# Other hold times for the exponential and the sines of the state-space parameters

## The chip, the cores and the metric

The kernel runs on one core of a Trainium2 chip. The metric is the device time of one execution in microseconds (us), lower is better. Inside a core five engines work side by side, each through its own queue in order: TensorE (PE; its weight loads are shown as PEld), VectorE (DVE), ScalarE (ACT), GpSimd (POOL) and SyncE (SP), which here only starts DMA transfers.

## The reference

The reference is a trunk of two decoder layers over 256 tokens of width 2048, in float32. Each layer normalises the input, multiplies it by one wide input matrix, and hands the columns to three mixers: a latent attention (MLA), a diagonal complex state-space layer (S5), and a dilated window attention. Their outputs are normalised, go through an output matrix, and are followed by a gated feed-forward part. What matters here is the discretisation of the state-space layer, whose parameters have 32 values per partition for both layers:

```
lam  = complex(min(a_re, -1e-4), a_im)
dt   = exp(log_dt)
a_bar = exp(lam * dt)
b_bar = ((a_bar - 1) / lam) * b
h_t  = a_bar * h_(t-1) + b_bar * u_t        # associative scan over the tokens
y    = Re(c . h) + d_skip * u
```

So the real part of `lam * dt` needs an exponential, and its imaginary part, an angle, needs sines and cosines.

## The kernel before, in words

**Matrix products.** Every weight matrix is cut into stripes of up to 512 columns. A stripe is accumulated over row blocks k of 128 rows. For accuracy each operand is split into a high and a low half, and one row block takes six products on TensorE: three for each of the two token halves. Weights come by DMA in tiles of two row blocks (512 KB for a full stripe, ring `wr` of 4 buffers). ACT copies a tile into its high half `wh`, DVE subtracts to get the low half `wl` (method `wsplit`, rings of 4 buffers each). The loop in `run` keeps the splits three tiles ahead of the products. A stripe's accumulators `acc` are emptied when it ends (`done`).

**Order of layer 0.** `ORDER[0]` starts with the stripe `cq` (16 row blocks, tiles 0 to 7) and the stripe `u` (tiles 8 to 15), then `ckv`. `cq_done` queues four ACT instructions (a copy and a sum of squares for each token half); the transposes of that copy (group `latq0`) follow on TensorE inside the stripe `u`. `u_done` starts the state-space chain, group `ssm0`, which also needs the parameters of group `prep0`. Its result is wanted by the stripes `g1` and `g0`, near the end of the layer's mixers.

**The planner.** The whole program is one fixed order per engine, written out when the kernel is built. Class `Pace` carries a clock for each engine (lines 113 to 182) and adds a cost for each instruction: for POOL 2.5 ns for each of the 32 columns plus 165 ns, and 450 ns more while the planner's DVE clock is ahead of its POOL clock (line 141), with 90 ns between dependent POOL instructions (line 143). Side work is written as generators. Each `yield` gives the earliest planner time of the next step. Before each row block, `run_side` (line 289) issues a step if its time has come on the planner's TensorE clock and the engines aren't `busy` (line 281): in layer 0 DVE may be ahead of TensorE by at most 3500 ns, ACT by at most 4500 ns. These clocks decide the order alone; on the chip each engine takes its queue in that order and waits where an operand isn't there.

**The parameters.** `params` (line 467) first issues 76 POOL instructions at once, at the very start of the kernel. They produce, in this order: `x` (the exponent's argument), `f`, `fh`, `fl` (the angle in turns), a half-angle sine and cosine by polynomials, `d` (the squared modulus of `lam`), and last `fr` (the angle's fraction for 128 tokens). The rest stands behind three yields:

```
480        mid = self.pace.t["gpsimd"] + Pace.LAG        # x is done
518        yield max(mid, self.HOLD[0])
519        self.pexp(nc.vector, E, x, W[21:25], em1)
520        yield max(early, self.HOLD[1])                # early: fl is done
521        yield from self.angles(0, 0)
522        yield max(late, self.HOLD[2])                 # late: fr is done
523        nc.vector.reciprocal(d, d)
525        nc.scalar.activation(s8, fr, AF.Sin, scale=2 * math.pi)
527        nc.scalar.activation(c8, fr, AF.Sin, bias=self.halfpi, scale=-2 * math.pi)
528        self.sines(0)
```

`pexp` is 17 small DVE instructions, `angles` three steps of DVE instructions, and the step behind the third yield holds one DVE reciprocal, six ACT instructions (four sines and two absolute values, the first with a table load) and 16 POOL products that end in `cr` and `ci`. The next step of `prep0` issues two loads on SP (`load_c`, `load_b`), then `ssm_c` and `ssm_b` follow on DVE and ACT.

Of the kernel before, what the change touches and what calls it, by code (L numbers as in the profile page):

```python
# [207 lines left out]
class Trunk:  # L208
# [46 lines left out]
        self.side.append([gen, group, self.pace.end + Pace.TO_PE if ready is None else ready])  # L255

    WARM = (9, 10)
    HOLD = (27000.0, 0.0, 39000.0)

    TUNE = (dict(W=3, s=10000.0, d=12000.0, m=9000.0, AV=3500.0, AS=4500.0, SL=0.0),  # L260
            dict(W=2, s=7000.0, d=16000.0, m=4000.0, AV=3000.0, AS=3000.0, SL=150.0))
# [205 lines left out]
    def params(self):  # L467
# [49 lines left out]
        late = self.pace.t["gpsimd"] + Pace.LAG  # L517
        yield max(mid, self.HOLD[0])
        self.pexp(nc.vector, E, x, W[21:25], em1)
        yield max(early, self.HOLD[1])  # L520
        yield from self.angles(0, 0)
        yield max(late, self.HOLD[2])
        nc.vector.reciprocal(d, d)
# [891 lines left out]
```

## Time and profile before

| | |
|---|---|
| median of 3 runs | 2173.07 us (2170.6 to 2173.99) |
| the profiled execution, device time | 2171.57 us |
| its span, first to last instruction | 2169.8 us |
| TensorE busy | 2127.0 us, 98% |
| VectorE busy | 1314.2 us, 61% |
| ScalarE busy | 1048.0 us, 48% |
| GpSimd busy | 96.3 us, 4%, most of it in the first 60 us |
| mean granted TensorE clock | 0.995 of full speed |

An engine's rows give when an instruction started and how long it ran; a bracket gives the idle time just before it and what ended it. The names are those of the program without their numbers: `wr`, `wh`, `wl` are the weight tile and its halves, `pt` and `acc` PSUM tiles, `one` a tile that lives through the kernel, `s` all other tiles in SBUF.

### The profile page before, as it was taken

The numbers are of one execution on the slowest core, as the hardware profiler recorded it, in microseconds if no ns is written. First come the engines' busy times: TensorE is split into PE (matmuls) and PEld (weight loads), VectorE is DVE, ScalarE is ACT, GpSimd is POOL, SyncE is SP. The second block draws the span as 40 slices with busy tenths as digits, with TensorE's granted clock in tenths as the row PEclk, the third lists the DMA queues.
The fourth block names the chain that finished last, engine by engine and source line by source line (L and its number), as shares of the span: only waits on it lengthen the run. The fifth ranks groups of instructions, "written<-read, shape, count | busy, mean of one in ns | idle before, by whom it ended". The sixth has DMA issues, their size and how long they took to land.

```text
span 2169.8 us, 27761 instructions
## 1 busy us (share of the span) xinstructions
PE 2127.0 (98%) x10511; PEld 1765.5 (81%) x10511; DVE 1314.2 (61%) x1789; ACT 1048.0 (48%) x1529; POOL 96.3 (4%) x251
## 2 busy tenths in 40 slices
PE   9999979999999999999999999999999999999998
PEld 7887768888888888888888887888888888888886
DVE  7996767458544555445568785765545455544555
ACT  6667445446334444444455665564443444434443
POOL 7100000000000000000001000000000000000000
PEclk9999999999999999999999999999999999999999
DMA  7653435667666666666555444566666766666664
GB/s 239 190 168 116 143 101 167 200 195 232 190 193 190 192 186 194 195 187 191 184 159 153 126 128 137 176 182 191 179 196 194 212 183 194 192 194 193 184 186 145
DMA packets 201269, 388.41 MB, mean 179 GB/s; under 512 B 12064, under 2 KB 20512, under 8 KB 201136
## 3 DMA queue, kind: packets, MB, share of 16 engines
q1 hardware_dynamic: 199952, 382.39, 58.4%
q0 software_dynamic: 1184, 4.26, 0.6%
q8 instruction: 82, 1.34, 0.3%
q14 instruction: 51, 0.42, 0.1%
HBM read 384.51 MB, written 2.10 MB: 178 GB/s over the span
## 4 chain that ended last, share of the span: by engine, by line
PE 87%; DVE 5%; ACT 3%; POOL 2%; issue 2%; DMA 0%; DVEq 0%; ACTq 0%; POOLq 0%
PE acc L198 82%; PE pt L198 5%; DVE s L198 3%; ACT s L198 2%; DVE wl L198 2%; POOL s L198 1%; PE y L198 1%; ACT wh L198 1%; POOL one L198 0%; DVE tn L198 0%; DMA wr<-in_w_ukv_dram 0%; POOL tn L198 0%; DMA one<-in_params_dram 0%; ACT L198 0%; DVE one L198 0%
## 5 line engine op out<-in xcount | busy, mean ns | idle before, releaser
L198 PE MATMUL acc<-wh,s 128*128 128x512 f32 (+2 forms) x5760 | 1808.6, 390 | 12.7 <-ACT s L198 7.9
L198 DVE TENSOR_TENSOR wl<-wr,wh 128x1024 fp32r<-128x1024 f32 (+1 forms) x720 | 866.2, 1209 | 679.2 <-ACT wh L198 677.0
L198 PEld LDWEIGHTS acc<-wh,s 128*128 128x128 f32 x5760 | 1079.3, 188 | 231.3 <-ACT s L198 9.9
L198 PE MATMUL acc<-wl,s 128*128 128x512 f32 (+2 forms) x2880 | 1114.6, 387 | 3.7 <-DVE wl L198 3.7
L198 ACT ACTIVATE wh<-wr 128x1024 fp32r<-128x1024 f32 (+1 forms) x720 | 747.9, 1047 | 730.4 <-PE acc L198 701.4
L198 PEld LDWEIGHTS acc<-wl,s 128*128 128x128 f32 x2880 | 542.0, 188 | 109.1 <-DVE wl L198 6.2
L198 ACT ACTIVATE s<-pt 128x512 fp32r<-128x512 f32 (+5 forms) x122 | 65.0, 549 | 137.1 <-PE pt L198 136.8
L198 DVE TENSOR_TENSOR s<-pt,s 128x512 f32<-128x512 f32 (+1 forms) x108 | 71.1, 686 | 59.2 <-ACT s L198 54.2
L198 PE MATMUL pt<-one,s 128*128 128x128 f32 x668 | 98.1, 273 | 3.4 <-DMA s<-in_x_dram 1.5
L198 ACT ACTIVATE s<-s 128x512 f32<-128x512 f32 (+4 forms) x162 | 79.9, 503 | 44.2 <-DVE s L198 35.5
L198 PEld LDWEIGHTS pt<-one,s 128*128 128x128 f32 x668 | 81.0, 142 | 23.8 <-ACT s L198 3.1
L198 DVE TENSOR_TENSOR s<-s,s 128x512 f32<-128x512 f32 (+3 forms) x88 | 78.0, 905 | 4.7 <-ACT s L198 4.0
L198 ACT ACTIVATE s<-pt,tn 128x128 f32<-128x128 f32 (+2 forms) x128 | 44.1, 375 | 75.9 <-DVE tn L198 58.8
L198 ACT ACTIVATE s<-acc,one 128x512 f32<-128x512 f32 (+3 forms) x112 | 63.3, 608 | 28.1 <-PE acc L198 22.9
L198 ACT ACTIVATE s<-pt,one 128x256 fp32r<-128x256 f32 x108 | 45.9, 470 | 63.6 <-PE pt L198 63.4
L198 DVE SCALAR_TENSOR_TENSOR s<-pt,one,s 128x256 fp32r<-128x256 f32 x108 | 47.7, 478 | 43.5 <-ACT s L198 43.1
L198 DVE SCALAR_TENSOR_TENSOR s<-acc,one,s 128x512 f32<-128x512 f32 x92 | 64.5, 743 | 10.0 <-POOL one L198 10.0
L198 PE MATMUL pt<-s,s 128*128 128x128 f32 (+1 forms) x352 | 58.2, 296 | 3.8 <-ACT s L198 2.7
L198 PEld LDWEIGHTS pt<-s,s 128*128 128x128 f32 x352 | 49.9, 191 | 9.2 <-ACT s L198 4.5
L198 POOL TENSOR_TENSOR tn<-one 128x2 f32<-128x2 f32 x27 | 10.9, 402 | 1027.1 <-DVE one L198 1025.7
L198 DVE TENSOR_TENSOR_SCAN s<-s,s 128x512 f32<-128x512 f32 x32 | 38.8, 1218 | 0.3
L198 DVE TENSOR_TENSOR s<-acc,s 128x512 f32<-128x512 f32 (+1 forms) x57 | 36.3, 673 | 3.9 <-PE acc L198 3.9
(74 smaller groups left out, 396.5 us busy)
## 6 DMA issues: line engine op xcount, KB each, us to landing
wr<-in_w_gate_dram SPq DMA_DIRECT2D x176, 512.0 KB, 4.2
wr<-in_w_up_dram SPq DMA_DIRECT2D x176, 512.0 KB, 4.2
wr<-in_w_down_dram SPq DMA_DIRECT2D x176, 512.0 KB, 4.3
wr<-in_w_in_dram SPq DMA_DIRECT2D x80, 512.0 KB, 4.1
wr<-in_w_o_dram SPq DMA_DIRECT2D x64, 512.0 KB, 3.9
wr<-in_w_uq_dram SPq DMA_DIRECT2D x16, 384.0 KB, 3.6
wr<-in_w_in_dram SPq DMA_DIRECT2D x16, 320.0 KB, 3.1
s<-in_bT_dram SPq DMA_DIRECT2D x8, 512.0 KB, 5.0
```

The lines of the kernel that those rows point to most:

```text
L198: return f(out, *a, **k)
```

## The change

One line: the three hold times behind which `params` keeps its later steps. The first, for the exponential, goes from 27000 to 16000 ns of the planner's clock. The third, for the reciprocal and the sines, goes from 39000 to 0, so that `late`, the planner's own estimate of when `fr` is done, decides. The second was 0 and stays 0.

```diff
     WARM = (9, 10)
-    HOLD = (27000.0, 0.0, 39000.0)
+    HOLD = (16000.0, 0.0, 0.0)
```

No instruction is added or taken out by it. What each engine does first can change, from the exponential on.

## Rows read from the trace of the kernel before

**Rows 1.** The page, busy time of each engine over the span.
```profile
PE 2127.0 (98%) x10511; PEld 1765.5 (81%) x10511; DVE 1314.2 (61%) x1789; ACT 1048.0 (48%) x1529; POOL 96.3 (4%) x251
```
**Rows 2.** Stretches: length, then PE, PEld, DVE, ACT, POOL busy us (count), clock, DMA.
```profile
54.00:61.00 7.00, 7.00 (x41) 6.34 (x40) 6.78 (x14) 4.13 (x7) 5.65 (x10) 1.00 0.75 276
160.00:200.00 40.00, 38.97 (x250) 32.85 (x250) 22.69 (x47) 28.66 (x77) 1.94 (x6) 1.00 0.43 131
```
**Rows 3.** Timeline of POOL: start, us, instruction, count, and idle time before it.
```profile
6.00 0.30 POOL L198 TENSOR_SCALAR one<-one 128x32 f32<-128x32 f32 x1 [4.05 <-DMA one<-in_params_dram]
...
16.96 0.47 POOL L198 TENSOR_TENSOR s<-one,s 128x32 f32<-128x32 f32 x2
...
21.40 2.37 POOL L198 TENSOR_SCALAR one<-s 128x32 f32<-128x32 f32 x1
...
24.82 0.29 POOL L198 TENSOR_SCALAR s<-s 128x32 f32<-128x32 f32 x1
...
42.85 0.32 POOL L198 TENSOR_SCALAR s<-s 128x32 f32<-128x32 f32 x1
```
**Rows 4.** Timeline of ACT around the sines.
```profile
32.52 1.06 ACT L198 ACTIVATE wh<-wr 128x1024 fp32r<-128x1024 f32 x1 [1.65 <-PE acc L198]
34.56 0.69 ACT L198 ACTIVATE s<-acc,one 128x512 f32<-128x512 f32 x1 [0.98 <-DVE s L198]
...
36.62 0.63 ACT L198 ACTIVATE s<-s 128x512 f32<-128x512 f32 x1
...
41.57 1.28 ACT L198 ACT_TABLE_LOAD   x1
43.20 0.23 ACT L198 ACTIVATE one<-s 128x32 f32<-128x32 f32 x1 [0.35 <-POOL s L198]
...
45.76 1.04 ACT L198 ACTIVATE wh<-wr 128x1024 fp32r<-128x1024 f32 x1
```
**Rows 5.** Timeline of DVE around the exponential, and the last split before the sines.
```profile
19.69 1.65 DVE L198 SCALAR_TENSOR_TENSOR s<-pt,one,s 128x256 fp32r<-128x256 f32 x4
21.26 2.35 DVE L198 TENSOR_TENSOR wl<-wr,wh 128x1024 fp32r<-128x1024 f32 x2
...
31.34 0.66 DVE L198 TENSOR_SCALAR s<-s 128x32 f32<-128x32 f32 x3
...
35.23 1.23 DVE L198 TENSOR_TENSOR wl<-wr,wh 128x1024 fp32r<-128x1024 f32 x1
...
41.42 1.23 DVE L198 TENSOR_TENSOR wl<-wr,wh 128x1024 fp32r<-128x1024 f32 x1
```
**Rows 6.** Timeline of PE, the places that the steps are moved past.
```profile
24.39 0.39 PE L198 MATMUL acc<-wl,s 128*128 128x512 f32 x1
...
39.13 0.60 PE L198 MATMUL pt<-one,s 128*128 128x128 f32 x4
...
40.73 0.63 PE L198 MATMUL acc<-wh,s 128*128 128x512 f32 x2
```
**Rows 7.** Timeline of PE, waits behind the change; all waits of 60 to 90 us over 0.5.
```profile
62.14 0.41 PE L198 MATMUL acc<-wl,s 128*128 128x320 f32 x1 [0.55 <-DVE wl L198]
...
82.65 0.73 PE L198 MATMUL acc<-wh,s 128*128 128x512 f32 x2 [1.53 <-DVE s L198]
```
**Rows 8.** The clock after a short and after a longer gap of PE: stretches and PE's timeline.
```profile
82.00:84.00 2.00, 1.35 (x6) 1.14 (x7) 2.00 (x6) 1.32 (x2) 0.00 (x0) 1.00 0.62 198
230.00:232.00 2.00, 0.49 (x4) 0.16 (x2) 2.00 (x3) 1.64 (x9) 0.00 (x0) 1.00 0.00 0
232.00:234.00 2.00, 1.22 (x2) 0.50 (x2) 1.97 (x3) 0.54 (x3) 0.00 (x0) 0.53 0.69 165
...
238.00:240.00 2.00, 2.00 (x10) 1.58 (x9) 0.12 (x1) 1.84 (x3) 0.11 (x1) 0.77 0.03 8
...
232.60 0.80 PE L198 MATMUL acc<-wh,s 128*128 128x512 f32 x1 [2.10 <-ACT s L198]
...
299.10 2.36 PE L198 MATMUL y<-s,one 128*32 128x128 f32 x40 [6.81 <-DVE s L198]
```

## The prediction, made before the change was run

> **What bounds the kernel now.** I read the page first: TensorE is busy for 2127.0 of 2169.8 us [rows 1], so all other engines matter only where TensorE waits for them, about 43 us in all. Then came the timelines of the first 60 us, engine by engine, since the change touches nothing else directly. After the start-up, TensorE's first wait is the one before 62.14 [rows 7]. POOL works through the 76 parameter instructions from 6.00 to 43.17 us [rows 3]. ACT sets its sines behind the high halves of tile 12, loads the table at 41.57 and waits 0.35 us for POOL's last value `fr` until 43.20 [rows 4]. DVE does the exponential at 31.34, when it is two tiles ahead [rows 5]. So now the sines arrive almost exactly when POOL is done, and nobody is kept waiting. The reader is to see that arrival: any earlier place in ACT's queue is a wait until about 43 us.
>
> **Where the planner puts the steps now.** This is order, not time, and I carried the planner's clocks by hand from the cost lines. At 245 ns an instruction plus 90 ns between dependent ones its POOL chain has `x` at 11.3, `fl` at 15.4 and `fr` at 27.4 us of its clock, far ahead of the 43.17 of the chip [rows 3]. A row block counts 1.362 us. The exponential may now go from 16.0 on; at 16.77 DVE is 3.60 us ahead, more than the 3.5 allowed, so it goes in at 18.13, in front of `cq`'s row block 5 and of the low half of tile 4 (before: in front of block 12). It adds 3.26 us to the DVE clock; row block 8, which needs tile 4, is thereby planned 2.6 us late. The three `angles` steps then fit in front of blocks 9, 11 and 13, and the sines in front of block 15, at 34.34 (before: `u`'s block 5, at 40.36). On ACT that is ahead of the high half of tile 10 and of the four `cq` instructions; on TensorE the transposes of `cq` now come in front of `u`'s block 4 (before: block 3).
>
> **Cost of the exponential.** DVE finishes the last input splits at 21.34 and starts two low halves at 21.26 [rows 5]; the exponential slips in between. It takes 31.34 to 35.23, 3.9 us [rows 5], and `x` is there at 17.43 [rows 3]. So tile 4's low half runs from 25.15 instead of 21.26 and ends at 26.4. Its first product runs at 24.39 now [rows 6]: TensorE waits **2.1 us**. Where the exponential stood, DVE was ahead, so nothing is won back there.
>
> **Cost of the sines.** ACT copies tile 9 one tile (2.7 us) ahead of tile 10, whose copy starts at 32.52 [rows 4]; with the first wait, 2.1, and the copy, 1.06, it is through at about 33, loads the table, and waits for `fr`. Behind the first sine stand, in ACT's queue, tile 10's high half, `cq`'s four instructions and all later tiles; behind those DVE's low halves, and on TensorE the `cq` transposes and then block 4 of `u`. When is `fr` done? A POOL instruction takes 0.29 us, but 2.37 while DVE makes two low halves [rows 3, 5]: each low half costs POOL (2.37 - 0.29) / 2 = 1.04. From 21.26 to 41.42 there are eight of them before `fr` (the first and the last stand in [rows 5]); with ACT standing, tiles 4 to 9 leave six. I take 43.17 - 2 x 1.04 = 41.1. Bounds: 43.2 if POOL gains nothing, and 43.17 - 8 x 1.04 = 34.9 if no low half met it.
>
> The Trainium skill (SBUF — State Buffer, Who interferes with whom) calls this an exclusive lock for which DVE with two SBUF inputs and POOL compete, and the one that issues later "fully blocks". By that rule the exponential's and the angles' DVE instructions would hold POOL as well; but both kernels run them ahead of `fr`, so only the two low halves count, as above; were the long POOL rows chance and no lock, `fr` would stay at 43.2 and the sum below would be 2.1 higher.
>
> From `fr` on: the six ACT instructions take 43.20 to 45.76, 2.56; tile 10's high half about 0.95 until the next can start (1.04 long); `cq`'s two copies with the first sum of squares 34.56 to 36.62, 2.06 [rows 4]; the transposes 0.4 [rows 6]. TensorE goes on at 41.1 + 2.56 + 0.95 + 2.06 + 0.4 = 47.1. Now block 4 starts with the second instruction of the row at 40.73, at about 40.95, with the transposes of 39.13 already behind it [rows 6]. The slip is **6.1 us**, with bounds 8.2 (POOL not faster) and 2.1 (the exponential alone). The two waits don't add: the second ends at a time that ACT sets, so the first, 2.1, lies inside the 6.1 and the second wait is 4.0. The table load of 1.28 us, on ACT's path either way, hides inside ACT's wait.
>
> **Cost of the clock.** After a gap of 1.53 us the granted clock stayed at 1.00, full speed or 2.4 GHz; after one of 2.10, with little work just before, it was 0.53, about 1.2 GHz, and back only in the stretch from 238 [rows 8]. With a 0.50 in the four microseconds between, the shortfall is (0.47 + 0.50 + 0.50 + 0.23) x 2 = 3.4 us of full-speed time, of which some 0.4 fell into gaps. I take **3.0 us** after the 4.0 us wait and none after the 2.1. Bounds 0 and 6 (both).
>
> **What is won back.** The moved step's 16 POOL products, and the two SP loads and DVE's `ssm_c` and `ssm_b` behind it, move with it. POOL's products and SP's loads lie beside other work (POOL is idle after 60 us [rows 1]; the loads only swap places with weight tiles, whose buffers are full while TensorE stands), and would cost their length if a weight tile came late. By planner slots `ssm_c` comes about three row blocks earlier, seen from TensorE. Now it runs while DVE is busy for 6.78 of 7 us [rows 2], and the waits over 0.5 us that follow until 90 are 0.55 for a low half and 1.53 for a DVE result [rows 7]. I take these two as gone: **-2.1 us**; bounds 0 and about -12 (the fast rival).
>
> **Sum.** 6.1 + 3.0 - 2.1 = +7.0. The profiled execution took 2171.57 us of device time, 1.8 above its span and 1.5 below the median of 2173.07; I add the change to the median: **2180.1 us**, +0.32%. Measurement can tell about 0.2% of this kernel, 4.3 us, from no change.
>
> **Rivals.**
> - *Nothing is won back and POOL isn't faster.* DVE is crowded until 160 us whatever its order, and POOL's last instructions may meet low halves by chance. 8.2 + 3.0 = +11.2: 2184.3. For it speaks that tile 10's halves, `cq` and the later tiles all queue up when ACT resumes.
> - *The clock falls at the first gap.* At 2.1 us it is as long as the one after which it fell [rows 8], though with full work before it. TensorE then loses 3 us by block 4, but it would have waited there anyway: the second gap shrinks to about 1 and the clock stays. 6.1 - 2.1 = +4.0: 2177.1, or less with more won back; within 0.2%.
> - *Faster: the state-space chain ends sooner.* At 299.10 TensorE has waited 6.81 us for that chain's last DVE result, and the clock was low afterwards [rows 8]: some 9.8 us with a clock loss of 3. If three row blocks of lead (4.1 us) and the emptier DVE survive until there, those go; with the clock held at 47 us that makes 6.1 - 2.1 - 9.8 = -5.8: 2167.3. It decides once the wins outweigh the 6.1 by 4.3 us. Against it: from 160 to 200 us DVE is busy for only 22.69 of 40 [rows 2], so there the chain isn't held by DVE's load but by the planner's turns, and a lead is easily lost.
> - *The change moves nothing on the chip*, since the limit on DVE's lead holds the steps back anyway: 2173. The step in front of block 14 misses the limit by 0.05 us, but then block 15 follows; the order of ACT's queue is the same.
>
> **How the numbers follow.** Forecast (slip, clock, two waits back) 0.42, of it 0.36 above 2177.4; the dearer rival 0.18; clock at the first gap, or more won back, 0.28, of it 0.04 above 2177.4; faster 0.10; nothing moves 0.02. Slower by over 0.2%: 0.36 + 0.18 + 0.04 = 0.58; same 0.06 + 0.24 + 0.02 = 0.32; faster 0.10. The range takes in the dearer rival and all of the cheap clock case, and leaves out the deeper part of the fast one: 2170 to 2185.
>
> **What would show it.** In the changed profile: the exponential on DVE at about 21.3 and a wait of TensorE for a low half of about 2 us near 24.4; ACT's table load near 34 and a first sine near 41 whose wait names POOL, 6 us or more long; a wait of TensorE of about 4 us that ends near 47 on ACT; a clock of 0.5 in the stretches after it; the waits of 62 and 82 us gone. Wrong would be: sines that still stand behind tile 12's copy, POOL done near 36, or a later wait of over 5 us that disappears or appears in layer 0 until 330 us, where the order of all side work may come out otherwise.

## The result, and the profile after

The changed kernel takes **2192.57 us** (median of 4 runs, 2191.11 to 2194.15), the kernel before 2173.53 us in the same comparison. The ratio is 1.0086, 95% interval 1.0074 to 1.0099: 19.0 us slower, where 7.0 were forecast. The sign was right, and the time lies outside the range. The profiled execution of after has a span of 2192.3 us, and a mean granted clock of 0.989.

The page of after, busy time of each engine. It answers [rows 1]: TensorE's busy time grew by 12.3 us without one more instruction (its clock was lower), and the rest of the profile's 22.5 us is in waits. ACT has two instructions less, 1527 for 1529: the program is the same, but its new order needs six table loads where the old one has eight (1.28 us each). So ACT has 2.6 us less to do in the new order, not more.

```profile
PE 2139.3 (98%) x10511; PEld 1776.4 (81%) x10511; DVE 1314.0 (60%) x1789; ACT 1045.6 (48%) x1527; POOL 91.9 (4%) x251
```

**The start-up.** The timeline of POOL in after, beside [rows 3] (start, us, instruction, count). The last row is the last value `fr`, which ended at 43.17 before; the long rows between stand beside DVE's low halves:

```profile
21.30 0.31 POOL L198 TENSOR_SCALAR one<-s 128x32 f32<-128x32 f32 x1
...
25.27 1.02 POOL L198 TENSOR_TENSOR s<-s 128x32 f32<-128x32 f32 x1
26.38 1.14 POOL L198 TENSOR_SCALAR s<-s 128x32 f32<-128x32 f32 x1
27.61 1.03 POOL L198 TENSOR_TENSOR s<-s 128x32 f32<-128x32 f32 x1
...
40.83 0.33 POOL L198 TENSOR_SCALAR s<-s 128x32 f32<-128x32 f32 x1
```

The timeline of ACT, beside [rows 4]; the bracket is the idle time ahead of an instruction, and what ended it:

```profile
33.36 1.28 ACT L198 ACT_TABLE_LOAD   x1
41.18 0.23 ACT L198 ACTIVATE one<-s 128x32 f32<-128x32 f32 x1 [6.54 <-POOL s L198]
...
43.73 1.04 ACT L198 ACTIVATE wh<-wr 128x1024 fp32r<-128x1024 f32 x1
```

The timeline of DVE, beside [rows 5]:

```profile
21.16 0.60 DVE L198 TENSOR_SCALAR s<-s 128x32 f32<-128x32 f32 x3
...
24.95 3.57 DVE L198 TENSOR_TENSOR wl<-wr,wh 128x1024 fp32r<-128x1024 f32 x3
...
44.80 1.23 DVE L198 TENSOR_TENSOR wl<-wr,wh 128x1024 fp32r<-128x1024 f32 x1 [5.42 <-ACT wh L198]
```

The timeline of TensorE. The rows up to 47.28 answer [rows 6], the last two [rows 7]; three stretches around 48 us answer [rows 8] (length, then PE, PEld, DVE, ACT, POOL busy and count, granted clock, DMA share, GB/s):

```profile
26.24 0.50 PE L198 MATMUL acc<-wl,s 128*128 128x512 f32 x1 [1.84 <-DVE wl L198]
...
45.40 0.33 PE L198 MATMUL pt<-one,s 128*128 128x128 f32 x1 [2.73 <-ACT s L198]
46.73 0.90 PE L198 MATMUL pt<-one,s 128*128 128x128 f32 x3 [1.00 <-ACT s L198]
47.28 0.78 PE L198 MATMUL acc<-wh,s 128*128 128x512 f32 x1
...
70.27 0.41 PE L198 MATMUL acc<-wl,s 128*128 128x320 f32 x1 [1.03 <-DVE wl L198]
...
89.55 0.73 PE L198 MATMUL acc<-wh,s 128*128 128x512 f32 x2 [1.42 <-DVE s L198]
```

```profile
46.00:48.00 2.00, 1.27 (x5) 1.18 (x6) 0.03 (x1) 1.97 (x6) 1.32 (x6) 0.61 0.43 69
48.00:50.00 2.00, 2.00 (x7) 1.57 (x6) 1.59 (x2) 2.00 (x5) 0.00 (x0) 0.54 0.51 194
50.00:52.00 2.00, 2.00 (x10) 1.63 (x9) 2.00 (x4) 1.00 (x2) 0.00 (x0) 1.00 0.55 95
```

Here the forecast holds. The exponential runs at 21.16, the first sine waits 6.54 us for POOL until 41.18, and TensorE resumes block 4 of `u` at 47.28 instead of about 40.95. By then the kernel is some 6.3 us late.

**The other half.** From here on I follow one marker through all kernels: the start of a stripe's first product, or of a named product, on TensorE's timeline. "Late" is its start less its start in before. In after the stripe `ckv` is 7.7 us late and `v`, at 169 us of before, 7.8 us. In between the delay falls to 5.4 us (at `p3`) and comes back, so nothing is won or lost on the whole between about 50 and 170 us. Then `m0`, at 211 us, is 5.6 us late, `m1` 12.1, `m3` 17.8, `d` 18.4, and the feed-forward part of layer 0 is 20.2 us late. Layer 1 adds 2.4 us more. So **12.4 us arise between `v` and the feed-forward part**, all of them behind 211 us, where the attention and the state-space layer are finished and which my sum did not touch.

TensorE's waits from 200 to 360 us, grouped by what they waited for (us in total, times, longest). Before:

```profile
PE y L198 <- DVE s L198: 6.8, 1, 6.8
PE acc L198 <- ACT s L198: 5.9, 3, 2.8
PE pt L198 <- ACT s L198: 1.5, 3, 0.7
PE acc L198 <- ACT wh L198: 1.2, 1, 1.2
...
```

After:

```profile
PE acc L198 <- ACT s L198: 7.2, 3, 2.7
PE pt L198 <- ACT s L198: 6.6, 5, 3.1
PE y L198 <- DVE s L198: 5.3, 1, 5.3
PE pt L198 <- DVE s L198: 2.1, 2, 1.4
...
```

The wait that I had as the price of the fast rival, 6.8 us for the state-space chain, shrank only to 5.3. A new kind took its place: transposes and products of the attention (`pt`) that wait 6.6 us for ACT, where it was 1.5. The stretch 200 to 360 us as a whole (length, then PE, PEld, DVE, ACT, POOL busy and count, granted clock, DMA share, GB/s), before:

```profile
200.00:360.00 160.00, 141.43 (x838) 115.33 (x837) 117.53 (x212) 76.29 (x168) 8.04 (x31) 0.95 0.41 129
```

and after:

```profile
200.00:360.00 160.00, 135.49 (x772) 110.46 (x771) 104.04 (x190) 69.15 (x159) 8.03 (x31) 0.89 0.35 112
```

TensorE stands for 24.5 instead of 18.6 us, and its clock is 0.89 instead of 0.95.

**What became of the order.** Two products show it: the first read-out of the state-space layer (`y`) and the first score of the latent attention (`pt` from a bf16 mask). Before:

```profile
94.73 1.30 PE L198 MATMUL y<-s,one 128*32 128x128 f32 x40
...
160.07 0.34 PE L198 MATMUL pt<-one 128*128 128x384 bf16 x1
```

After:

```profile
108.54 1.30 PE L198 MATMUL y<-s,one 128*32 128x128 f32 x40
...
146.71 0.34 PE L198 MATMUL pt<-one 128*128 128x384 bf16 x1
```

While the stripes around them are 5.5 to 8 us late, the state-space layer is 13.8 us late, thus 6 to 8 us behind its old place, and the attention begins 13.4 us sooner, thus 21 us ahead of its old place. The change names only the exponential and the sines. But the planner takes each step when its turn comes. In the written order of the two programs the later parameter steps (of the second to the fourth chunk) stand 2 to 22 row blocks sooner, most of the state-space steps 2 to 7 blocks later, and the latent attention's mostly 4 to 18 blocks sooner. The first cause the second: in the third run below (both early, order of before) only the later parameter steps are held back, and the state-space and attention steps are then written at exactly their old places. That they do it by using up the 3500 ns by which DVE may lead is read from the planner's rule, and no run tests it.

### The profile page after: what moved, and what is told of

It reads as the page before. It is cut to its first block, busy times and chain, and to the rows that moved or that the text cites. A ratio compares the mean times of both kernels' runs of the same rounds, so it can differ in the third digit from the quotient of the medians.

```text
span 2192.3 us, 27742 instructions
## 1 busy us (share of the span) xinstructions
PE 2139.3 (98%) x10511; PEld 1776.4 (81%) x10511; DVE 1314.0 (60%) x1789; ACT 1045.6 (48%) x1527; POOL 91.9 (4%) x251
## 4 chain that ended last, share of the span: by engine, by line
PE 88%; DVE 5%; ACT 2%; POOL 2%; issue 2%; DMA 1%; DVEq 0%; ACTq 0%; POOLq 0%
PE acc L198 82%; PE pt L198 5%; DVE s L198 3%; ACT s L198 2%; DVE wl L198 2%; POOL s L198 1%; PE y L198 1%; ACT wh L198 1%; DVE tn L198 1%; POOL tn L198 0%; DMA wr<-in_w_ukv_dram 0%; DMA one<-in_params_dram 0%; DMA wr<-in_w_in_dram 0%; POOL one L198 0%; DVE one L198 0%
## 5 line engine op out<-in xcount | busy, mean ns | idle before, releaser
L198 PEld LDWEIGHTS acc<-wh,s 128*128 128x128 f32 x5760 | 1082.3, 189 | 232.2 <-ACT s L198 11.1
L198 PE MATMUL pt<-one,s 128*128 128x128 f32 x668 | 101.3, 277 | 12.1 <-ACT s L198 10.1
L198 DVE SCALAR_TENSOR_TENSOR s<-acc,one,s 128x512 f32<-128x512 f32 x92 | 64.6, 743 | 10.2 <-POOL one L198 10.2
```

Source lines behind the costliest of these rows:

```text
L198: return f(out, *a, **k)
```

## The experiments

Theory R: the loss at 200 to 360 us comes from the rewritten order, and the early sines and exponential by themselves cost only the 5 to 8 us of the start-up (the first 50 us). Theory S: it comes from the sines' wait and what that delays. All times are medians, and each is compared with runs of before on the same chip; "+" is the difference from these.

| kernel | median, us | against before | ratio, 95% interval |
|---|---|---|---|
| the change | 2192.57 | +19.0 | 1.0074 to 1.0099 |
| exponential early alone | 2187.16 | +13.8 | 1.005 to 1.008 |
| sines early alone | 2173.52 | +0.2 | 0.9993 to 1.0011 |
| both early, order of before behind them | 2180.65 | +7.3 | 1.0019 to 1.0042 |
| start-up of before, order of after | 2187.0 | +13.6 | 1.0047 to 1.0077 |
| start-up of after, later parameter steps early | 2182.34 | +9.5 | 1.0026 to 1.0052 |
| later parameter steps early, alone | 2173.33 | +0.7 | 0.9995 to 1.0013 |
| parameter and state-space steps at after's places | 2181.97 | +9.3 | 1.0023 to 1.0052 |
| attention steps at after's places | 2192.19 | +19.4 | 1.0071 to 1.0101 |
| before, waits filled with zero products | 2169.27 | -3.5 | 0.9976 to 0.9995 |
| after, waits filled | 2185.69 | +12.9 | 1.0042 to 1.0075 |

**Exponential early alone**

```diff
-    HOLD = (27000.0, 0.0, 39000.0)
+    HOLD = (16000.0, 0.0, 39000.0)
```

> Only the first hold is lowered (16000, 0, 39000): the exponential stands at its early place, the sines are held to 39000 again. The planner then writes out all side work from the u stripe on in the changed kernel's order, though the sines wait little. Theory R (the order of the side work, rewritten because the parameter steps come sooner, makes the loss; the start-up costs about 5 to 8 of the 20 us): the exponential's wait of 2 us plus 13 to 16 us in the stretch from 200 to 360 us, +14 to +18 over the kernel before, about 2189. Theory S (the sines' wait at the start is what costs, directly and by what it delays): +2 to +4, about 2176.

Measured: 2187.16 us, +13.8. The sines keep their hold, `ckv` is only 2.6 us late, and still the kernel ends 19.2 us late in its profile, which is of the slowest of its four executions. The delay is 0.8 at `m0`, 11.1 at `m3`, 7.0 at `g1` and 16.9 at the last of the `d` stripes. The two products named above are at 104.26 and 142.43 us: the order of after. So the larger part of the loss needs no early sine. Theory R holds, a little below its size.

**Sines early alone**

```diff
-    HOLD = (27000.0, 0.0, 39000.0)
+    HOLD = (27000.0, 0.0, 0.0)
```

> Only the third hold is lowered (27000, 0, 0). By the planner's clocks the sines then move by a single row block (u's block 4 instead of 5), since the angles before them and the limit on DVE's lead hold them anyway, and all later side work keeps the order of the kernel before. Theory R: 0 to +1.5, about 2174. Theory S: the wait for POOL at the new place, one block earlier, about 1.4 us of ACT time, and what follows from it: +1 to +6.

Measured: 2173.52 us, no difference, as theory R has it. With the exponential where it was, the steps behind it fill the time until 39000 ns anyway; the sines move by one row block. These products stand at 94.31 and 159.70 us, as before.

**Both early, the order of before behind them.** The yield behind the sines is given a time of its own, late enough that the rest finds the turns that it has in before:

```diff
         self.sines(0)
...
-        yield
+        yield 49400.0
```

> The changed kernel with one more hold behind the sines (the next parameter step not before 49400 on the planner's clock). The start-up is that of the changed kernel to the instruction, both waits included; from u's block 10 on the side work has the order of the kernel before. Theory R: only the start-up's cost, which the changed kernel's trace shows as a slip of 7.7 us at the stripe ckv: +5 to +8, about 2180. Theory S: +17 to +20, about 2192.

Measured: 2180.65 us, +7.3. TensorE's timeline in this kernel, the first read-out, the first score and the read-out with the long wait:

```profile
102.97 1.30 PE L198 MATMUL y<-s,one 128*32 128x128 f32 x40
...
168.35 0.34 PE L198 MATMUL pt<-one 128*128 128x384 bf16 x1
...
308.05 2.36 PE L198 MATMUL y<-s,one 128*32 128x128 f32 x40 [6.81 <-DVE s L198]
```

All three are later than in before by 8.2 to 9.0 us, and the wait is the same 6.81 us [rows 8]. What happens at the start is carried to the end: 8.5 us at `ckv`, 9.9 at the end of the profile; no later wait takes any of it up. This is the size of the start-up by itself.

**The start-up of before, the order of after.** Here the side steps of the kernel follow a written list: the exponential, the angles and the sines as in before, all that comes behind them as in after. Two kinds of step ahead of the sines stand as in after too, three steps of the input's splitting two row blocks later and the transposes of `cq` one; `ckv` is 0.2 us late with them. No instruction of the program is added or left out.

```diff
     def run_side(self):
-        again = True
-        while again:
...
+        self.call += 1
+        for n in STEPS.get(self.call - 1, ()):
+            self.step(next(s for s in self.side if s[3] == n))
```

> The other half: the exponential, the angles and the sines at the places of the kernel before (no early waits), and all later side work in the order of the changed kernel, written out as a fixed list of steps. Theory R: the loss of the stretch from 200 to 360 us without that of the start, +11 to +15, about 2187. Theory S: 0 to +3, about 2175.

Measured: 2187.0 us, +13.6. TensorE's timeline: the first read-out, the first score, the new wait of the attention, and the last read-out.

```profile
102.54 1.30 PE L238 MATMUL y<-s,one 128*32 128x128 f32 x40
...
140.71 0.34 PE L238 MATMUL pt<-one 128*128 128x384 bf16 x1
...
228.71 0.89 PE L238 MATMUL pt<-one,s 128*128 128x128 f32 x3 [3.57 <-ACT s L238]
...
307.90 2.36 PE L238 MATMUL y<-s,one 128*32 128x128 f32 x40 [4.92 <-DVE s L238]
```

`ckv` is 0.2 us late and `m0` even 0.7 early, then `m1` is 3.4, `g0` 9.1 and `d` 10.2 us late. The two halves, 7.3 and 13.6, make 20.9 beside the 19.0 of the change; the intervals, each about 2.5 to 3.5 us to either side, allow the difference. Theory R holds, S falls.

The next runs ask **which part of the order** costs. All use such lists, taken from before, with the places of after for one group of steps.

**Later parameter steps early** (with the start-up of after). The list for this kernel also moved the exponential and the sines, contrary to what its expectation says.

> The kernel before, its start-up and its order, except that the remaining steps of the state-space parameters (the second, third and fourth chunk's loads, angles, sines and splits) stand at the places that the changed kernel gives them, 3 to 20 row blocks sooner; the state-space and attention steps stay where they were. Theory 'crowding': these 20-odd steps cost by themselves, since DVE gets them while it is behind with the weight splits. Then this kernel alone gives most of the 13.6 us: 2181 to 2187 us. Theory 'displacement': they cost nothing themselves, and what counts is what is put in their old places. Then it stays near the kernel before: 2171 to 2176 us.

Measured: 2182.34 us, +9.5. `ckv` is 9.8 us late and everything behind it until layer 1 between 8.8 and 9.4; the long wait is 6.82 us. That is the run with both early over again (+7.3), within the intervals. The next one leaves the start-up out.

> The kernel before with the later parameter steps (second to fourth chunk) alone at the changed kernel's places; unlike in e5_param_steps_early, where the exponential and the sines went along with them, these two stay where the kernel before has them. Theory 'displacement' (these steps cost nothing by themselves, the 9 us of e5_param_steps_early are its start-up): 2171 to 2175 us, all waits of 200 to 360 us within 0.5 us of the kernel before. Theory 'crowding': 2179 us or more.

Measured: 2173.33 us, +0.7, no difference; the waits of 6.82, 2.77 and 2.10 us are those of before. By themselves the parameter steps cost nothing at the places of after. 'Crowding' falls.

**Parameter and state-space steps at after's places**

> The kernel before, its start-up included, with the later parameter steps and the state-space steps of layer 0 (most of these 2 to 6 row blocks later) at the changed kernel's places; the attention steps stay where the kernel before has them. Theory 'attention' (the loss comes from the attention steps that stand earlier, so that TensorE, in order, waits for their chain through DVE and ACT): 2171 to 2176 us. Theory 'both': the later state-space chain costs too, and the wait ahead of its product at 299 us is longer than 6.81 us: 2178 to 2184 us.

Measured: 2181.97 us, +9.3. TensorE's last read-out in layer 0, and the stretch in which it stands (columns as above), in which TensorE is busy for less than half of the time and at a clock of 0.57:

```profile
308.04 2.36 PE L243 MATMUL y<-s,one 128*32 128x128 f32 x40 [7.98 <-DVE s L243]
```

```profile
300.00:320.00 20.00, 9.31 (x65) 7.11 (x62) 13.11 (x22) 4.80 (x9) 0.00 (x0) 0.57 0.13 47
```

'Both' is right: a state-space chain that is 7.3 us late at its first read-out (101.99 against 94.73) costs by itself. The wait went from 6.81 to 7.98 us only; the rest is spread, with `m0` 5.0, `m3` 7.5 and `d` 10.3 us late.

**Attention steps at after's places**

> The kernel before, its start-up and its order, except that the steps of the latent and the dilated attention of layer 0 stand at the places that the changed kernel gives them (the latent attention's mostly 2 to 20 row blocks sooner, some of the last ones later); parameter and state-space steps stay. Theory 'attention': the 13.6 us come from the attention's steps, which now crowd ACT and DVE at the state-space chain's cost: 2180 to 2187 us, with the chain's wait at 299 us longer or a new wait of 3 us near 229 us. Theory 'late chain': they come from the state-space steps that stand 2 to 6 row blocks later; then this kernel is near before: 2170 to 2176 us, and the wait of 6.81 us ahead of the state-space product at 299 us stays within 1 us of that.

Measured: 2192.19 us, +19.4, as much as the whole change and more than the whole order of after. 'Late chain' falls; 'attention' has the direction and a size that is 5 us too small. Its three engines at the longest wait that before hasn't; the second row is the wait ahead of the state-space product, 6.81 us before. TensorE:

```profile
241.05 1.15 PE L242 MATMUL pt<-one,s 128*128 128x128 f32 x3 [6.29 <-ACT s L242]
...
313.69 2.36 PE L242 MATMUL y<-s,one 128*32 128x128 f32 x40 [7.38 <-DVE s L242]
```

ACT:

```profile
235.00 1.05 ACT L242 ACTIVATE wh<-wr 128x1024 fp32r<-128x1024 f32 x1
240.54 0.37 ACT L242 ACTIVATE s<-pt,tn 128x128 f32<-128x128 f32 x1 [4.48 <-DVE tn L242]
```

DVE:

```profile
236.09 1.23 DVE L242 TENSOR_TENSOR wl<-wr,wh 128x1024 fp32r<-128x1024 f32 x1 [1.80 <-ACT wh L242]
237.23 2.48 DVE L242 TENSOR_TENSOR s<-s,s 128x1024 f32<-128x1024 f32 x2
239.62 0.62 DVE L242 TENSOR_REDUCE tn<-pt 128x1 f32<-128x128 f32 x2
```

From the bottom up: the maxima of a softmax (`tn<-pt`) stand in DVE's queue behind a weight split, for which DVE waits 1.80 us, and behind two state-space products, 2.48 us together. ACT's exponential waits 4.48 us for them, and TensorE, whose next instruction is the transpose of that softmax, 6.29 us. Another of 5.92 us is at 162.02. Nothing here is long by itself: TensorE, which takes its queue in order, has the attention's next product at a point where DVE still has other work ahead of the attention's. The changed kernel has the same chain at 234.67: its ACT waits 2.09 us for `tn`, which DVE makes behind the split of 232.11, and TensorE 3.15:

```profile
234.67 1.14 PE L198 MATMUL pt<-one,s 128*128 128x128 f32 x3 [3.15 <-ACT s L198]
```

The parts don't add: attention alone +19.4, parameters and state space alone +9.3, all together (with a few steps of the feed-forward's input, which only that kernel moves) +13.6. It may be that the two chains keep some of their spacing when they move together, and that each runs into the other when it moves alone; no run shows it.

**The waits filled.** Products that add zero to the open accumulator (or start the tile that comes next) are put ahead of TensorE's longest waits, each group 0.3 us or so shorter than the wait: 57 of 512 columns in before, 62 and 52 short ones of 128 in after. The profile lacks some of their records, so that its rows below count 7 and 28 where 8 and 29 were issued.

```diff
+            if self.name == "tensor":
+                if self.count in FILL:
...
+                    for _ in range(int(FILL[self.count] / (0.418 * w))):
+                        self.eng.matmul(o[:, :w].bitcast(F32), m[:, 4], m[:, 0:w // 128].rearrange("p a b -> p (a b)"),
...
+                self.count += 1
```

> The kernel before with products that add zero, on TensorE, ahead of six of its waits between 230 and 331 us (2.10, 0.96, 6.81, 2.77, 1.08, 1.23 us), each group 0.3 us shorter than the wait by the full clock. They keep TensorE at work while it would wait. Theory 'clock': the half clock behind each wait, 8.6 us summed over 200 to 360 us, is caused by the pause, and goes: 2165 to 2168 us, with the clock of 200 to 360 us at 0.98 or more. Theory 'clock is not the pauses' (it comes from the small products of the drains): 2172 to 2176 us, the clock as before.

Measured: 2169.27 us, -3.5: faster than before, by 0.15%. The stretch as a whole, and TensorE around the first and the third group:

```profile
200.00:360.00 160.00, 150.74 (x900) 118.90 (x905) 118.65 (x213) 77.20 (x169) 8.10 (x31) 1.00 0.43 132
```

```profile
231.29 1.67 PE L204 MATMUL acc<-one 128*128 128x512 bf16 x7
233.35 0.50 PE L212 MATMUL acc<-wh,s 128*128 128x512 f32 x1 [0.39 <-ACT s L212]
...
291.90 6.21 PE L204 MATMUL acc<-one 128*128 128x512 bf16 x28
298.67 1.30 PE L212 MATMUL y<-s,one 128*32 128x128 f32 x40 [0.56 <-DVE s L212]
```

> The changed kernel with products that add zero, on TensorE, ahead of seven of its waits between 234 and 351 us (3.15, 1.90, 1.89, 5.31, 2.71, 2.56, 1.26 us). If the half clock, 17.4 us summed over 200 to 360 us against 8.6 in the kernel before, follows from the pauses, most of it goes and only the 5.8 us of longer waits and the start-up's 6 stay: 2177 to 2183 us. If the clock does not follow from the pauses: 2191 to 2196 us. The difference from the kernel before with the same filling is then the waits' alone: 12 us by the first theory, 19 by the second.

Measured: 2185.69 us, +12.9 where after has +19.0: 6.1 us came back. Its clock over 200 to 360 us is 0.99. 'Clock' is right about the cause: the pauses make the clock fall, since it stays full when they are filled (the read-out takes 1.30 instead of 2.36 us, [rows 8]). It is wrong about the size, by which the two kernels would have taken at most 2168 and 2183 us. A clock of 0.95 and 0.89 over 160 us is 8 and 17.6 us of full-speed time, and only 3.5 and 6.1 came back. Much of the half clock falls into waits and ahead of waits: in before the read-out of 299.10 was 1.06 us slower and then TensorE waited 2.77 us for ACT anyway; in the filled kernel that wait is filled with 2.3 us and 0.29 more. Between the two filled kernels there are still 16.4 us. So by the medians the clock explains about 2.6 of the 19 us, by the two pairs of profiles (22.5 less 14.1) about 8; between these the runs don't decide. The larger part is waits either way. The fillers can also cost something themselves: in both kernels the last group waited over 1.1 us for DVE before it could start.

## Why the prediction was right or wrong

- **Where the planner puts the first steps: right.** The exponential at 21.16 us (21.3 forecast), the sines ahead of tile 10's copy, the table load at 33.36 (34).
- **The exponential's cost: right.** TensorE waits 1.84 us for tile 4's low half (2.1).
- **The sines' cost: right.** `fr` comes at 41.16 (41.1): POOL was done 2.0 us sooner, for 2.08 forecast from two low halves fewer. From 21.3 us to `fr` each of the eight low halves of before and of the six of after has a POOL instruction beside it that takes 1.0 to 1.2 us (the pair at 21.26 one of 2.37), and every other one there takes at most 0.52; beside the exponential's small DVE instructions it is 0.22 to 0.33 us in both kernels. The lock that the Trainium skill tells of (SBUF — State Buffer, Who interferes with whom) agrees with these rows; the 1.04 us for a low half is from the rows, not from the page. TensorE resumes block 4 at 47.28 (47.1): 6.3 us late for 6.1, in two waits of 2.73 and 1.00 for my one of 4.0.
- **The clock: mechanism right, half the size.** It fell behind the second gap and not behind the first, as forecast. It was 0.61 and 0.54 in the stretches of 46 and 48 us and full from 50: 1.7 us of shortfall, for 3.0. The 3.0 was copied from [rows 8], where the clock was low for twice as long.
- **What is won back: wrong, and this is the step that failed.** I had the moved steps shorten the two next waits (0.55 and 1.53 us, [rows 7]). They are 1.03 and 1.42 in after: nothing is won there. Between `ckv` and `p3` 2.2 us come back, but they are lost again by `k`. Worse, I treated the steps behind the sines as a lead that is either kept or lost, a term between 0 and -12. It was none. With the early steps gone, the planner gave all later steps other turns: the rest of the parameters sooner, the state-space steps later, the attention's sooner, so that TensorE stood for attention products that DVE and ACT didn't have ready. The run with the order of after and the start-up of before prices that at **+13.6 us**, with the sign that I had excluded for this term.
- **The sum without that step.** 6.1 + 3.0 = 9.1 against 7.3 measured with the old order behind the early steps. In after, 7.8 us until `v`, 12.4 until the feed-forward part and 2.4 in layer 1 are, but for rounding, the 22.5 us by which the profile of after is longer than that of before; the medians differ by 19.0.
- **The rivals.** The dear one (+11.2) assumed the right thing about what is won back, and the wrong thing about POOL. The fast one had the right place, 299 us, and the wrong sign: the chain's first read-out comes later, not sooner, since the state-space steps stand later in the order. I wrote that the order of all side work may come out otherwise, but as what would make me wrong and without a price. The sign that I gave for it, a wait of over 5 us that comes or goes, didn't show: the 6.81 us became 5.31, and the new waits are of 1 to 3 us. It deserved a chance and a price: the change makes a greedy planner go on from another state, and the range should have had an end well above +11.2.

## What to carry to other kernels

In a kernel whose order comes out of a greedy planner, moving one step moves everything behind it. Price the local effect and the new order as two terms, the second with a wide range: here the waits of the stretch that it changed were 18.6 us, and the new order cost 13.6, almost twice the local effect of 7.3. None of the orders tried here gained anything. To tell the two apart, make the step early but hold what follows at its old turn, and replay the new order behind the old start. For a chain over several engines look at what stands ahead of its links in each queue: bringing it forward only on TensorE's list makes TensorE wait.

## What the runs showed of the hardware

- Products that add zero keep TensorE's clock full through a wait of 6.8 us (1.00 over 160 us, where it was 0.95). This gave 3.5 us (interval 1.1 to 5.2), and a kernel faster than both.
- A shortfall of the granted clock is not lost time one for one. Of 8 and 17.6 us, 3.5 and 6.1 came back.
- A delay of 8 to 10 us from the first 58 us stays to the end to within 1.5 us when the order behind it is the same, or the same but for the later parameter steps (8.5 to 9.9 us in the one run, 9.8 to 8.6 in the other): no later wait took it up.
- The order of ACT's queue decides how many table loads it holds: eight with the order of before, six with that of after, 1.28 us each.

What stays open: which of the attention's steps must not come earlier, and why moving all together costs less than moving the attention alone. No run splits the attention's steps. Of the 2.4 us of layer 1 this much shows: its steps have the same order in both kernels and TensorE's waits there are as long (6.6 us in all, 6.8 before), but the clock was 0.98 from 1100 to 1200 us and 0.99 from 1300 to 1420, where it was 1.00 before. The run with the sines early alone, as fast as before, has the 0.99 there too, so part of it may come and go with the execution.
